# Gate one-hots from bf16 comparisons over eight tokens, in a hybrid conv / RWKV-7 / PEER layer

## The chip, the cores and the metric

The kernel runs on one core of one Trainium2 chip, as one launch. The metric is the device time of that core in microseconds (us). Besides plain runs there is one profiled execution, whose trace is read here. Engines are called by the profile's names: PE (matmuls), PEld (weight loads), DVE (VectorE), ACT (ScalarE), POOL (GpSimd), SP (the queue that issues most DMAs). "L1028" is line 1028 of the kernel before.

## The reference, cut to what matters

One layer for 1024 tokens of width 1024. A token-mixing sub-layer (convolution heads and an RWKV-7 recurrence) is followed by PEER retrieval over 128 x 128 = 16384 single-neuron experts. The change lies in the second part:

```
q  = (h2 @ peer_wq) per head (8 heads), split into two halves
s1 = q[:half] . peer_k1   (128 keys)      s2 = q[half:] . peer_k2   (128 keys)
v1, i1 = top_k(s1, 16);   v2, i2 = top_k(s2, 16)
sc, ci = top_k(all 256 sums v1[i] + v2[j], 16)
experts = i1[ci // 16] * 128 + i2[ci % 16];   gates = softmax(sc)
z   = h2 . peer_u[experts];   act = gelu(z) * gates
y2  = sum over the 8 x 16 chosen experts of act * peer_v[experts]
```

So each token has 128 chosen experts, each with a first key (0 to 127), a second key (0 to 127) and a gate.

## The kernel before

**Two ways through PEER.** Tokens are cut into eight tiles of 128. Tiles 5, 6, 7 (`GT`) gather their chosen rows by indirect DMA. Tiles 0 to 4 (`DT`, 640 tokens) go the dense way: all 16384 experts are computed by matmuls, and the result is multiplied by a gate matrix that is zero except at the chosen experts. The gate matrix of a token is 128 x 128 (first key by second key). It is built as a product of two one-hot matrices over the 128 choices k of the token: `oa[k, e] = (first key of k == e)` and `ob[k, e] = gate of k * (second key of k == e)`; a matmul over k gives the matrix.

**Stages.** First the input projection and the convolution; then the RWKV recurrence over 16 chunks, into which other work is filled in as generators (`fill`); then what is left of that work; last, from about 1380 us on, the dense experts (line 1250 on: 32 groups with matmuls at L1268 and L1302) with the gathers beside them. The work filled in, in order of its emission: `front` (output projection and norms of 256 tokens), `query` (query projection, scores, and `best16`: top 16 on DVE), `choose` (from the two top 16 to experts and gates of one tile, on the list `slow`), and `gate_matrix` (list `gates`, one step per four tokens). Lines 600 and 1111 set how often a gate step is emitted; a scheduler orders each engine's instructions by emission and priority, and gate steps after the recurrence get a raised priority (`GPRI`).

**choose** (L917). Positions become keys by a lookup as a one-hot sum: `oh = (iota_q == sel)` (L968, bf16), times the key (L971), summed over 16 places. On POOL (`E is G`, the tiles below token 512) the sum is a tree of four adds (L977, L979); on DVE (`E is V`: tiles 4 and 5 here, and tiles 6 and 7 later in `choose_late`, two heads at a time) it is one reduction, L974. Keys and gates are stored as f32 in `sel_d` (L960), but for tile 4, whose tiles are handed over directly.

**gate_matrix** (L995). The three 128 x 128 arrays of a tile (first keys, second keys, gates; rows are tokens) are loaded into `selr` (L1006) and transposed on PE into one PSUM bank (L1012); ACT copies them to SBUF as `selt` (L1013) and negated as `selneg` (L1018). For four of the five tiles the bank (`selbank`) is kept for the tile and the keys are read from it in PSUM; for the first tile they are read from `selt` in SBUF. Then, for each four tokens ("a quad", 160 in all):

- DVE compares an f32 iota with the four first keys: `oa`, 512 elements (L1028), and with three second keys: `ob[:, :3]`, 384 elements (L1032).
- POOL multiplies these three by their gates (L1034).
- ACT makes the fourth from the iota alone: Square of (iota - key), then Relu of (gate - gate * square) (L1037, L1038).
- PE multiplies, one matmul per token (L1040), and ACT copies the result to `stage` (L1041). Each 32 tokens `stage` goes to DRAM (L1048), 2 MB at a time.

`oa` and `ob` are rings of `GB` = 3 buffers. Tiles of the stages before the experts are drawn from one ring of `NPAGE` = 31 pages of 2 KB per partition (`page`, L161).

Of the kernel before, what the change touches and what calls it, by code (L numbers as in the profile page):

```python
# [16 lines left out]
OP = mybir.AluOpType  # L17
# [48 lines left out]
RATES = 1.0, 1.0  # L66
NPAGE = 31
TSLOW = 2
TGATE = 12
CBUF = 4  # L70
GB = 3
ABUF = 6
# [13 lines left out]
def layer_kernel(ctx, tc, x, cols, c_row, cond_w, w_in, w2a2, g2, w_out, ln_rows, wq, keys, peer_u, peer_ut, peer_v, peer_vt, out):  # L86
# [16 lines left out]
    ident = const.tile([128, 128], F32)  # L103
    iota = const.tile([128, 128], F32)
    G.iota(iota, pattern=[[1, 128]], base=0, channel_multiplier=0, allow_small_or_imprecise_dtypes=True)
    eps_ln = const.tile([128, 1], F32)
# [19 lines left out]
    h2t_d = dram.tile([2, KD, 128, ND], F32, name="h2t_d")  # L126
    sel_d = dt([3, 128, 128], "sel_d", 8)
    score_d = {t: [dram.tile([128, 512], F32, name=f"score_d{t}_{g}") for g in range(4)] for t in range(6, 8)}
    split_d, fetched = {}, {}
# [787 lines left out]
    def choose(tt, val, idx, h0, nh, nb, new, E):  # L917
# [9 lines left out]
        for hh in range(0, nh, nb):  # L927
# [8 lines left out]
            for h in range(hh, hh + nb):  # L936
                best16(top[:, h], pos[:, h], cand[:, h - hh, :])
                yield

        place = pos.bitcast(I32)  # L940
        V.tensor_scalar(m1, place, 32.0, None, op0=OP.is_ge)
# [17 lines left out]
        yield  # L959
        put = lambda w, t: None if tt == DT[-1] else ld(sel_d[tt][w][:, h0 * TOPK:h0 * TOPK + n], t.rearrange("p h r -> p (h r)"))  # L960
        for half, sel in ((0, isel), (1, jsel)):
            ib = qb[:, 2 + half]
            A.activation(ib, idx[:, :, half, :], AF.Copy)
            for hh in range(0, nh, nb):
                hs = slice(hh, hh + nb)
                oh = new("oh", BF, nb * TOPK * TOPK).rearrange("p (h q r) -> p h q r", h=nb, q=TOPK)
                sh4 = [128, nb, TOPK, TOPK]
                V.tensor_tensor(oh, iota_q[:, None].to_broadcast(sh4), sel[:, hs, None, :].to_broadcast(sh4),  # L968
                                op=OP.is_equal)
                yield  # L970
                E.tensor_mul(oh, oh, ib[:, hs, :, None].to_broadcast(sh4))  # L971
                yield
                if E is V:
                    V.tensor_reduce(fo[half][:, hs], oh.rearrange("p h q r -> p h r q"), axis=AX.X, op=OP.add)  # L974
# [20 lines left out]
    def gate_matrix(tt, chosen):  # L995

        three = lambda nm: gb[0].tile([128, 3, 128], F32, name=nm)
        quad_ = lambda nm: gb[0].tile([128, 4, 128], F32, name=nm, bufs=GB)
        st = three("selt")
        if chosen:  # L1000
            s = [t.rearrange("p h r -> p (h r)") for t in chosen]
        else:
            kept_ = three("selr")
            s = [kept_[:, w] for w in range(3)]
            for w in range(3):
                ld(s[w], sel_d[tt][w])  # L1006

        selbank.append(selbank.pop(0))
        pt = (selbank[0].tile([128, 512], F32, tag="mgate", name="selbank", bufs=1) if selbank[0] else mgate())[:, :384]
        pt = pt.rearrange("p (w t) -> p w t", w=3)  # L1010
        for w in range(3):
            T.transpose(pt[:, w], s[w], ident)  # L1012
        A.activation(st, pt, AF.Copy)  # L1013
        i1, i2, gt = (st[:, w] for w in range(3))
        if selbank[0]:
            i1, i2 = pt[:, 0], pt[:, 1]
        neg = three("selneg")
        A.activation(neg, pt, AF.Copy, scale=-1.0)  # L1018
        for r0 in range(0, 128, TB):
# [5 lines left out]
            for q in range(0, TB, 4):  # L1025
                ts = slice(r0 + q, r0 + q + 4)
                oa, ob = quad_("oa"), quad_("ob")
                V.tensor_tensor(oa, iota[:, None, :].to_broadcast([128, 4, 128]),  # L1028
                                i1[:, ts, None].to_broadcast([128, 4, 128]), op=OP.is_equal)
                pt = mgate().rearrange("p (t e) -> p t e", t=4)  # L1030

                V.tensor_tensor(ob[:, :3], iota[:, None, :].to_broadcast([128, 3, 128]),  # L1032
                                i2[:, ts.start:ts.start + 3, None].to_broadcast([128, 3, 128]), op=OP.is_equal)
                G.tensor_mul(ob[:, :3], ob[:, :3], gt[:, ts.start:ts.start + 3, None].to_broadcast([128, 3, 128]))  # L1034
                c, o = slice(ts.start + 3, ts.start + 4), ob[:, 3, :]

                A.activation(o, iota, AF.Square, bias=neg[:, 1, c])  # L1037
                A.activation(o, o, AF.Relu, bias=gt[:, c], scale=neg[:, 2, c])  # L1038
                for t in range(4):
# [17 lines left out]
    for c in range(16):  # L1057
# [3 lines left out]
        if c == 9:  # L1061
# [4 lines left out]
            fet.close()  # L1066
            gb.append(fex.enter_context(tc.tile_pool(name="gb", bufs=1)))
        if c < 14:
            flight.append([solve(c + 2)])
# [302 lines left out]
```

## Time and profile before

| what | value |
|---|---|
| three runs | 3225.85, 3225.45, 3225.2 us; median 3225.45 |
| profiled execution | 3225.41 us; its span in the trace 3223.5 us |
| granted TensorE clock, mean | 0.953 |
| busy, share of the span | PE 93%, PEld 80%, DVE 80%, ACT 37%, POOL 56% |
| L1028, 160 comparisons | 117.1 us of DVE, between 864 and 1400 us |
| L1032, 160 comparisons | 91.9 us of DVE |
| L974, 8 reductions, tiles 4 and 5 | 15.9 us of DVE, between 1316 and 1363 us |

The share of a whole span is an average over stages with different limits, so the prediction reads the stage in which the gate matrix is built: how busy each engine is there, and which wait ends last. Idle time of an engine that doesn't bind costs nothing. Rows with "x8" are groups of eight instructions; "<-" after a row's idle time names what released the engine.

### The profile page before, as it was taken

To read this page: it belongs to the slowest core of one execution; us is meant where nothing else is said; L and a number is where in the kernel's file an instruction comes from. 1 tells how busy PE (TensorE), PEld (TensorE's weight loads), DVE (VectorE), ACT (ScalarE), POOL (GpSimd) and SP (SyncE) were. 2 spreads that over 40 slices of the span, in tenths; PEclk is the share of its full clock that TensorE was granted. 3 is DMA by queue.
4 is the path that set the end of the run, shared out by engine and by line. 5 is a ranking of instruction groups with operands and counts; after the bars stand their busy time and mean duration, and the time that the engine had idled before them with its cause. 6 is when DMAs were issued, how large, how long until landed. Compare 5 with 4: busy or idle time off the path is not lost.

```text
span 3223.5 us, 53860 instructions
## 1 busy us (share of the span) xinstructions
PE 2995.2 (93%) x19952; PEld 2582.2 (80%) x19952; DVE 2563.2 (80%) x5612; ACT 1198.1 (37%) x2314; POOL 1796.7 (56%) x1408
## 2 busy tenths in 40 slices
PE   6968999899799589899999999999999999999995
PEld 4735677478688479899899988899989898999994
DVE  6279566856977979958999999898878777778788
ACT  5562344253353467552223232322323232222222
POOL 2410011133441853367777776787878777787872
PEclk9979899979699799999999999999999999999997
DMA  8876465378566898999999989899999999999994
GB/s 307 290 208 229 135 179 170 113 235 288 169 193 240 266 307 253 311 350 329 340 336 328 341 317 321 307 336 347 339 335 339 346 328 354 329 345 330 344 339 171
DMA packets 411782, 922.30 MB, mean 286 GB/s; under 512 B 81744, under 2 KB 221568, under 8 KB 389504
## 3 DMA queue, kind: packets, MB, share of 16 engines
q1 hardware_dynamic: 218688, 474.23, 43.2%
q0 software_dynamic: 110592, 402.70, 33.8%
q10 hardware_dynamic: 82240, 41.94, 4.6%
q8 instruction: 156, 2.56, 0.3%
q14 instruction: 106, 0.87, 0.1%
HBM read 788.91 MB, written 129.85 MB: 285 GB/s over the span
## 4 chain that ended last, share of the span: by engine, by line
PE 46%; DVE 13%; DMA 3%; issue 2%; ACT 1%; POOL 1%; SPq 0%; ACTq 0%; DVEq 0%; POOLq 0%
PE mg L1268 22%; PE md L1302 21%; DVE grow L1194 2%; PE mgate L1040 2%; DVE yacc L1307 1%; DVE gy L1201 1%; DMA vraw<-peer_vt 1%; PE mm L194 1%; DMA G_d<-stage 1%; DVE oa L1028 1%; DVE ob L1032 1%; DMA grow<-peer_v,eid 0%; DVE tkg L974 0%; DVE oh L968 0%; DVE bnst L202 0%
## 5 line engine op out<-in xcount | busy, mean ns | idle before, releaser
L1268 PE MATMUL mg<-h2h,uhi 128*128 128x320 f32 x2024 | 626.1, 309 | 8.0 <-DVE al L1274 8.0
L1268 PE MATMUL mg<-h2l,uhi 128*128 128x320 f32 x2024 | 625.1, 309 | 0.0
L1268 PE MATMUL mg<-h2h,ulo 128*128 128x320 f32 x2024 | 624.9, 309 | 0.0
L1201 DVE SCALAR_TENSOR_TENSOR gy<-grow,gz,gy 128x1024 f32<-128x1024 f32 x381 | 487.7, 1280 | 19.1 <-DMA grow<-peer_v,eid 17.3
L1302 PE MATMUL md<-vhi,al 128*128 128x512 f32 x1280 | 497.9, 390 | 0.0
L1302 PE MATMUL md<-vlo,ah 128*128 128x512 f32 x1280 | 496.5, 390 | 0.0
L1302 PE MATMUL md<-vhi,ah 128*128 128x512 f32 x1280 | 491.7, 391 | 4.1 <-DVE yacc L1307 2.1
L1194 DVE SCALAR_TENSOR_TENSOR grow<-grow,gh 128x1024 f32<-128x1024 f32 x384 | 460.6, 1210 | 25.6 <-DMA grow<-peer_u,eid 24.2
L1186 POOL DMA_INDIRECT grow<-peer_u,eid x384 | 363.1, 946 | 187.3 <-DVE grow L1194 78.4
L1186 POOL DMA_INDIRECT grow<-peer_v,eid x384 | 361.9, 942 | 187.6 <-DVE gy L1201 99.4
L1268 PEld LDWEIGHTS mg<-h2h,uhi 128*128 128x128 f32 x2024 | 379.9, 188 | 16.8 <-DVE al L1274 11.5
L1268 PEld LDWEIGHTS mg<-h2l,uhi 128*128 128x128 f32 x2024 | 379.9, 188 | 4.6
L1268 PEld LDWEIGHTS mg<-h2h,ulo 128*128 128x128 f32 x2024 | 379.9, 188 | 3.2
L1229 POOL TENSOR_TENSOR vlo<-vraw,vhi 128x1024 fp32r<-128x1024 f32 x128 | 309.0, 2414 | 32.4 <-ACT vhi L1227 30.0
L1229 POOL TENSOR_TENSOR ulo<-uraw,uhi 128x1024 fp32r<-128x1024 f32 x128 | 309.1, 2415 | 29.9 <-ACT uhi L1227 27.9
L1307 DVE TENSOR_TENSOR yacc<-md,yacc 128x512 f32<-128x512 f32 x310 | 210.6, 685 | 124.9 <-PE md L1302 124.3
L1302 PEld LDWEIGHTS md<-vhi,ah 128*128 128x128 f32 x1280 | 239.6, 188 | 53.1 <-ACT ah L1273 4.0
L1034 POOL TENSOR_TENSOR ob<-ob,selt 128x384 f32<-128x384 f32 x160 | 144.9, 907 | 241.7 <-DVE ob L1032 163.4
L1302 PEld LDWEIGHTS md<-vlo,ah 128*128 128x128 f32 x1280 | 240.3, 188 | 48.6
L1227 ACT ACTIVATE vhi<-vraw 128x1024 fp32r<-128x1024 f32 x128 | 135.2, 1056 | 387.8 <-DMA vraw<-peer_vt 369.9
L1302 PEld LDWEIGHTS md<-vhi,al 128*128 128x128 f32 x1280 | 240.3, 188 | 45.1 <-DVE al L1274 0.2
L182 POOL TENSOR_TENSOR wsplit<-wraw,wsplit 128x1024 fp32r<-128x1024 f32 x46 | 112.6, 2450 | 221.0 <-ACT wsplit L181 214.3
(404 smaller groups left out, 5916.8 us busy)
## 6 DMA issues: line engine op xcount, KB each, us to landing
uraw<-peer_ut SPq DMA_DIRECT2D x128, 512.0 KB, 7.1
vraw<-peer_vt SPq DMA_DIRECT2D x128, 512.0 KB, 5.5
wsplit<-split_wq SPq DMA_DIRECT2D x48, 1024.0 KB, 6.7
G_d<-stage ACTq DMA_DIRECT2D x20, 2048.0 KB, 13.6
gmat<-G_d SPq DMA_DIRECT2D x32, 1024.0 KB, 8.1
cw<-cond_w SPq DMA_DIRECT2D x48, 512.0 KB, 5.0
wsplit<-split_w_out SPq DMA_DIRECT2D x24, 1024.0 KB, 5.9
split_w_in<-wsplit SPq DMA_DIRECT2D x22, 1024.0 KB, 5.1
```

The lines of the kernel that those rows point to most:

```text
L182: G.tensor_sub(lo, raw, hi.bitcast(F32))
L194: T.matmul(pt, l[:, k, :], r[k], start=i == 0, stop=i == 3 * KD - 1)
L1034: G.tensor_mul(ob[:, :3], ob[:, :3], gt[:, ts.start:ts.start + 3, None].to_broadcast([128, 3, 128]))
L1040: T.matmul(pt[:, t, :], ob[:, t, :], oa[:, t, :], start=True, stop=True)
L1186: G.indirect_dma_start(out=r, out_offset=None, in_=peer_u if k < 128 else peer_v, in_offset=bass.IndirectOffsetOnAxis(ap=eid[:, k % 128:k ...
L1194: V.scalar_tensor_tensor(r, r, 1.0, ht, op0=OP.mult, op1=OP.mult, accum_out=z[:, i:i + 1])
L1201: V.scalar_tensor_tensor(y, r, z[:, i - 128:i - 127], y, op0=OP.mult, op1=OP.add)
L1227: A.activation(hi, raw, AF.Copy)
L1229: G.tensor_sub(lo, raw, hi.bitcast(F32))
L1268: T.matmul(p, l[:, k, :], r[k][:, bs], start=i == 0, stop=i == 3 * KD - 1)
L1302: T.matmul(p, l[:, ts], r[:, e % 2, :], start=e == 0 and q == 0, stop=e == 3 and q == 2)
L1307: ins = V.tensor_add(ya, p, ya)
```

## The change

It rewrites how the one-hots are made:

- `choose` for dense tiles writes the keys as bf16 (`fo` in `qb`) and stores them in a new bf16 array `keyb_d`. The sum over places is now the tree of adds on DVE too where a tile's eight heads are done at once; the reduction stays only in `choose_late`.
- `gate_matrix` loads bf16 keys and f32 gates into a slot of the `ob` ring, transposes the keys in bf16 into the bank, and keeps them there as bf16 (for the first tile a bf16 copy in SBUF, `selk2`). Only the gates are copied to SBUF; the negated copy goes.
- DVE compares a bf16 iota, laid out as expert by eight tokens (`iota_e`), with the keys of eight tokens: two comparisons of 1024 bf16 elements, `mask`, for eight tokens, one per key half.
- ACT copies four tokens of the first mask to f32 `oa`. POOL multiplies three tokens of the second mask with the gates into `ob`. ACT makes the fourth as a Copy with the gate as scale.
- `oa` has two buffers instead of three, `mask` has three; there are 30 pages instead of 31. The f32 iota moves out of the constants; for the masks a second one is made once, in a page.

```
-NPAGE = 31
+NPAGE = 30
-GB = 3
+GB = 2, 3
+MB = 3
...
+    keyb_d = [dram.tile([2, 128, 128], BF, name=f"keyb_d{i}") for i in range(8)]
...
+        dense = tt in DT
...
+        if dense:
+            fo = qb[:, 4], qb[:, 5]
...
-                if E is V:
+                if nh < NH:
                     V.tensor_reduce(fo[half][:, hs], oh.rearrange("p h q r -> p h r q"), axis=AX.X, op=OP.add)
                     continue
...
+            got = quad_("ob", GB[1]).rearrange("p t e -> p (t e)")
+            kb = got.bitcast(BF)[:, 0:256].rearrange("p (w k) -> p w k", w=2)
+            sg = got[:, 128:256]
+            k1, k2 = kb[:, 0], kb[:, 1]
+            ld(kb, keyb_d[tt].rearrange("w p k -> p w k"))
+            ld(sg, sel_d[tt][2])
...
+        keys_ = pt.bitcast(BF)[:, 0:256].rearrange("p (w k) -> p w k", w=2)
+        for w, k in enumerate((k1, k2)):
+            T.transpose(keys_[:, w], k, identb)
+        T.transpose(pt[:, 128:256], sg, ident)
+        gt = gb[0].tile([128, 128], F32, name="selt")
+        A.activation(gt, pt[:, 128:256], AF.Copy)
+        if not selbank[0]:
+            both = gb[0].tile([128, 2, 128], BF, name="selk2")
+            A.activation(both, keys_, AF.Copy)
+            keys_ = both
...
-                V.tensor_tensor(oa, iota[:, None, :].to_broadcast([128, 4, 128]),
-                                i1[:, ts, None].to_broadcast([128, 4, 128]), op=OP.is_equal)
+                if q % 8 == 0:
+                    masks = []
+                    for w in range(2):
+                        m = gb[0].tile([128, 128, 8], BF, name="mask", bufs=MB)
+                        V.tensor_tensor(m, iota_e, keys_[:, w, None, r0 + q:r0 + q + 8].to_broadcast([128, 128, 8]),
+                                        op=OP.is_equal)
+                        masks.append(m)
+                ma, mb = (m[:, :, q % 8:q % 8 + 4].rearrange("p e t -> p t e") for m in masks)
+                oa, ob = quad_("oa", GB[0]), quad_("ob", GB[1])
+                A.activation(oa, ma, AF.Copy)
+                c = r0 + q
+                G.tensor_mul(ob[:, :3], mb[:, :3], gt[:, c:c + 3, None].to_broadcast([128, 3, 128]))
+                A.activation(ob[:, 3], mb[:, 3], AF.Copy, scale=gt[:, c + 3:c + 4])
...
-                V.tensor_tensor(ob[:, :3], iota[:, None, :].to_broadcast([128, 3, 128]),
-                                i2[:, ts.start:ts.start + 3, None].to_broadcast([128, 3, 128]), op=OP.is_equal)
-                G.tensor_mul(ob[:, :3], ob[:, :3], gt[:, ts.start:ts.start + 3, None].to_broadcast([128, 3, 128]))
...
-                A.activation(o, iota, AF.Square, bias=neg[:, 1, c])
-                A.activation(o, o, AF.Relu, bias=gt[:, c], scale=neg[:, 2, c])
...
+            iota_e = gb[0].tile([128, 128, 8], BF, name="iota_e")
+            V.tensor_copy(iota_e, iota[:, :, None].to_broadcast([128, 128, 8]))
```

More of the change, by code (lines that the diff above doesn't have):

```diff
@@ L103, in layer_kernel @@
     ident = const.tile([128, 128], F32)
-    iota = const.tile([128, 128], F32)
-    G.iota(iota, pattern=[[1, 128]], base=0, channel_multiplier=0, allow_small_or_imprecise_dtypes=True)
     eps_ln = const.tile([128, 1], F32)
@@ L152, in layer_kernel @@
     iota_q = const.tile([128, TOPK, TOPK], BF, name="iota_q")
+    iota = fe.tile([128, 128], F32, name="iota")
+    G.iota(iota, pattern=[[1, 128]], base=0, channel_multiplier=0, allow_small_or_imprecise_dtypes=True)
     V.tensor_copy(iota_q, iota[:, :TOPK, None].to_broadcast([128, TOPK, TOPK]))
@@ L959, in choose @@
         yield
-        put = lambda w, t: None if tt == DT[-1] else ld(sel_d[tt][w][:, h0 * TOPK:h0 * TOPK + n], t.rearrange("p h r -> p (h r)"))
+        if dense:
+            fo = qb[:, 4], qb[:, 5]
+        put = lambda w, t: None if tt == DT[-1] else ld((keyb_d if dense and w < 2 else sel_d)[tt][w][:, h0 * TOPK:h0 * TOPK + n],
+                                                        t.rearrange("p h r -> p (h r)"))
         for half, sel in ((0, isel), (1, jsel)):
@@ L995, in gate_matrix @@
     def gate_matrix(tt, chosen):
-        three = lambda nm: gb[0].tile([128, 3, 128], F32, name=nm)
-        quad_ = lambda nm: gb[0].tile([128, 4, 128], F32, name=nm, bufs=GB)
-        st = three("selt")
+        iota_e, identb = gb[1:]
+        quad_ = lambda nm, bufs: gb[0].tile([128, 4, 128], F32, name=nm, bufs=bufs)
         if chosen:
-            s = [t.rearrange("p h r -> p (h r)") for t in chosen]
+            k1, k2, sg = [t.rearrange("p h r -> p (h r)") for t in chosen]
         else:
[L1003 to L1006, printed above, removed]
-        selbank.append(selbank.pop(0))
[L1009 to L1018, printed above, removed]
+            got = quad_("ob", GB[1]).rearrange("p t e -> p (t e)")
[4 more added lines that the diff above has]
+            ld(sg, sel_d[tt][2])
+        selbank.append(selbank.pop(0))
+        pt = selbank[0].tile([128, 512], F32, tag="mgate", name="selbank", bufs=1) if selbank[0] else mgate()
+        keys_ = pt.bitcast(BF)[:, 0:256].rearrange("p (w k) -> p w k", w=2)
[8 more added lines that the diff above has]
+            keys_ = both
         for r0 in range(0, 128, TB):
@@ L1067, in layer_kernel @@
             gb.append(fex.enter_context(tc.tile_pool(name="gb", bufs=1)))
+            iota = page("iota", w=128)
+            G.iota(iota, pattern=[[1, 128]], base=0, channel_multiplier=0, allow_small_or_imprecise_dtypes=True)
+            iota_e = gb[0].tile([128, 128, 8], BF, name="iota_e")
+            V.tensor_copy(iota_e, iota[:, :, None].to_broadcast([128, 128, 8]))
+            identb = gb[0].tile([128, 128], BF, name="identb")
+            V.tensor_copy(identb, ident)
+            gb.extend((iota_e, identb))
         if c < 14:
```

3 lines of the change are left out of this document (removed).

## The prediction, made before the changed kernel had run

> **What bounds the kernel now.** I read the page first for the shares, then the windows view, to find where VectorE (DVE) is the engine that is never idle, then the same windows for line 1028 alone, to see how much of the changed work lies in each. Columns of the first view: window, its length, busy us (and instructions) of PE, PE's weight loads, DVE, ACT and POOL, then the granted TensorE clock, the DMA share and GB/s.
>
> ```profile
> span 3223.5 us, 53860 instructions
> ```
> ```profile
> 300.00:820.00 520.00, 485.99 (x4634) 356.15 (x4632) 350.20 (x913) 204.64 (x412) 109.93 (x67) 0.90 0.60 191
> 820.00:1000.00 180.00, 160.16 (x1901) 140.41 (x1899) 153.46 (x486) 88.43 (x206) 84.06 (x83) 0.86 0.55 179
> 1000.00:1050.00 50.00, 45.31 (x389) 36.53 (x389) 37.07 (x215) 13.65 (x32) 7.10 (x7) 0.93 0.73 252
> 1050.00:1100.00 50.00, 25.43 (x125) 21.31 (x123) 49.72 (x140) 23.14 (x47) 39.46 (x36) 0.77 0.78 247
> 1100.00:1250.00 150.00, 126.85 (x925) 120.17 (x925) 125.97 (x389) 92.36 (x218) 83.69 (x89) 0.91 0.93 302
> 1250.00:1370.00 120.00, 105.15 (x849) 101.75 (x849) 118.58 (x362) 78.68 (x192) 45.49 (x46) 0.96 0.85 276
> 1370.00:1405.00 35.00, 33.02 (x260) 32.00 (x259) 19.50 (x35) 27.56 (x65) 17.14 (x19) 0.99 1.03 349
> 1405.00:3223.00 1818.00, 1770.31 (x9923) 1610.57 (x9921) 1516.71 (x2684) 515.92 (x847) 1342.92 (x1024) 0.99 0.91 328
> ```
>
> The last 1818 us are the expert matmuls, PE busy 97% of them; the change touches no instruction there. Everything is decided before 1405, where the gate matrix is built beside the last projections. DVE is full in two windows, 49.7 of 50 and 118.6 of 120. Between them (1100 to 1250) DVE has 24 us idle, and the DMA engines carry 0.93 of their time. At the end, PE (33 of 35) and DMA are full.
>
> Line 1028 runs once for four tokens (a "quad"), so its count says how many quads each window holds:
>
> ```profile
> 820.00:1000.00 180.00, 30.80 (x32) 0.86 0.55 179
> 1050.00:1100.00 50.00, 6.02 (x9) 0.77 0.78 247
> 1100.00:1250.00 150.00, 36.38 (x54) 0.91 0.93 302
> 1250.00:1370.00 120.00, 31.61 (x47) 0.96 0.85 276
> 1370.00:1405.00 35.00, 11.65 (x17) 0.99 1.03 349
> ```
>
> **The price of a comparison.** DVE's groups between 820 and 1405 us (line, engine, operation, out<-in, shapes, count | busy, mean ns | idle before), then a stretch of its timeline (start, us), then single lines (count: min/median/max ns, first and last start):
>
> ```profile
> L1028 DVE TENSOR_TENSOR oa<-iota,selbank 128x512 f32<-128x512 f32 x128 | 86.3, 674 | 28.0 <-PE mgate L1040 27.6 <-ACT selneg L1018 0.2
> L1032 DVE TENSOR_TENSOR ob<-iota,selbank 128x384 f32<-128x384 f32 x128 | 69.6, 544 | 0.0
> ```
> ```profile
> 1348.83 2.35 DVE L971 TENSOR_TENSOR oh<-oh,tkb 128x1024 bf16<-128x1024 bf16 x2
> 1351.10 0.67 DVE L1028 TENSOR_TENSOR oa<-iota,selbank 128x512 f32<-128x512 f32 x1
> 1351.70 0.54 DVE L1032 TENSOR_TENSOR ob<-iota,selbank 128x384 f32<-128x384 f32 x1
> 1352.16 2.98 DVE L971 TENSOR_TENSOR oh<-oh,tkb 128x1024 bf16<-128x1024 bf16 x2
> 1356.12 4.05 DVE L974 TENSOR_REDUCE tkg<-oh 128x64 f32<-128x1024 bf16 x2
> 1360.09 0.67 DVE L1028 TENSOR_TENSOR oa<-iota,selbank 128x512 f32<-128x512 f32 x1
> ```
> ```profile
> L1028 DVE TENSOR_TENSOR oa<-iota,selbank x128: 630/675/690, 1003.8 to 1399.1; 128x512 f32<-128x512 f32 x128
> ...
> L1028 DVE TENSOR_TENSOR oa<-iota,selt x32: 647/693/2415, 864.1 to 994.1; 128x512 f32<-128x512 f32 x32
> ```
> ```profile
> L968 DVE TENSOR_TENSOR oh<-iota_q,tkb x24: 677/684/2400, 824.1 to 1347.6; 128x1024 bf16<-128x1024 bf16 x24
> L968 DVE TENSOR_TENSOR loh<-iota_q,ltkb x16: 404/416/1252, 1540.9 to 2141.6; 128x512 bf16<-128x512 bf16 x16
> ```
>
> A quad costs DVE 1.06 us from start to start (1351.10 to 1352.16; neighbours overlap by 0.075 us), so eight tokens cost 2.12. After the change eight tokens cost two bf16 comparisons of 1024 elements. The trace has that shape twice. L968 compares a bf16 iota with bf16 keys that run contiguously, both in SBUF: 0.684 us (median), 0.61 after the overlap. L971 has an operand repeated along the innermost axis: 2.27 us for two (1348.83 to 1351.10), 1.135 each. So the same 1024 bf16 elements cost 0.61 or 1.135. The new comparison reads runs of eight contiguous keys and a contiguous iota, which is L968's pattern, but its keys lie in PSUM for four of the five tiles (selbank, 128 of the 160 quads), and no row of before has a bf16 operand in PSUM. An f32 comparison loses nothing by a PSUM operand: 675 ns with selbank, 693 with selt in SBUF (medians). I take 0.61 because the access pattern is L968's, and keep 1.135 as the other end. Saved per quad: (2.12 - 1.22)/2 = 0.45 us; at the other end (2.27 - 2.12)/2 = 0.075 us is lost.
>
> The Trainium skill speaks against this: "VectorE: DVE Perf Modes", section "The perf-mode tier table (the rule you actually need)", puts a tensor_tensor with any PSUM operand at one element per cycle. The section on PSUM operands below it caps them only at the packed two-element mode, and no run here shows which holds. By the tier table the sum would be the first rival's.
>
> **The lookup sums.**
>
> ```profile
> L974 DVE TENSOR_REDUCE tkg<-oh x8: 1972/2018/2109, 1315.8 to 1363.1; 128x64 f32<-128x1024 bf16 x8
> ```
>
> Eight reductions, 1.985 us each from start to start (1356.12 to 1360.09 is two), become four adds each on DVE, of 512, 256, 128 and 64 outputs. From the two L968 rows, 512 elements more cost 268 ns; so 0.416, 0.28, 0.215 and 0.18, less four overlaps: 0.80 us. But an add reads two SBUF tensors, and such instructions stretch beside POOL:
>
> ```profile
> L968 DVE TENSOR_TENSOR oh<-iota_q,tkb 128x1024 bf16<-128x1024 bf16 x8 | 6.9, 916 | 0.0
> ```
> ```profile
> L1034 POOL TENSOR_TENSOR ob<-ob,selt x160: 818/827/2817, 867.4 to 1400.4; 128x384 f32<-128x384 f32 x160
> ```
> ```profile
> 1308.64 2.35 DVE L971 TENSOR_TENSOR oh<-oh,tkb 128x1024 bf16<-128x1024 bf16 x2
> ...
> 1308.86 2.82 POOL L1034 TENSOR_TENSOR ob<-ob,selt 128x384 f32<-128x384 f32 x1 [3.53 <-DVE ob L1032]
> ```
>
> Between 1250 and 1370 L968 averages 0.916 us instead of 0.684, and the POOL multiply at 1308.86, usually 0.83 us, lasted 2.82 beside two L971. With 0.2 us more per add, a reduction's replacement costs 1.6; I take 0.38 saved, 3 us for the eight. Ends: 9.4 us saved (no collision), 4 us lost (each add waits for half a POOL multiply of 0.83 us). All eight lie in the window 1250 to 1370.
>
> **ACT and POOL.** ACT's groups between 820 and 1405, and the two rows nearest to its new work (ns min/median/max):
>
> ```profile
> L1041 ACT ACTIVATE stage<-mgate 128x512 f32<-128x512 f32 x160 | 94.7, 592 | 89.9 <-PE mgate L1040 83.3 <-DMA wsplit<-split_wq 6.2
> L1038 ACT ACTIVATE ob<-ob,selt,selneg 128x128 f32<-128x128 f32 x160 | 77.0, 494 | 17.5 <-DMA G_d<-stage 13.4 <-ACT ob L1037 1.2 <-DMA selr<-sel_d 1.0
> L1037 ACT ACTIVATE ob<-iota,selneg 128x128 f32<-128x128 f32 x160 | 62.9, 397 | 9.6 <-PE mgate L1040 9.4
> ```
> ```profile
> L486 ACT ACTIVATE ctap<-ident,colt x104: 381/389/403, 223.1 to 613.1; 128x128 f32<-128x128 f32 x104
> L800 ACT ACTIVATE ychi<-ycf x16: 612/630/633, 542.8 to 1109.7; 128x512 fp32r<-128x512 f32 x16
> ```
>
> Per quad ACT loses Square and Relu (0.397 + 0.494) and gains a 512-element copy (0.63, L800) and a Copy with a column scale (0.389, L486): 0.13 us more. In the window 1250 to 1370 that is 47 x 0.13 = 6 us on 78.7, under PE's 105; at nothing. If strided bf16 reads took ACT twice as long, it would be 0.76 per quad, 114 us, and ACT would bind; L1041 reads four strided tokens at the same 0.59 us as a dense copy, which speaks against it. The copy also puts ACT between DVE and the matmul, beside POOL's multiply of 0.83 us, which ends later. POOL's multiply keeps its 384 elements; only an operand turns bf16. The negated copy (L1018, five times) goes. iota_e, identb and the second iota are made once, about 2 us of DVE where it has 27 us idle (820 to 1000).
>
> **Loads and pages.** The three loads of a tile's selection become two, into a slot of the ob ring instead of a buffer of their own. The chain has, in order of time:
>
> ```profile
> 1141.75 3.98 PE mgate L1040 x18
> 1145.85 1.17 SPq L1006
> 1147.08 8.95 DMA selr<-sel_d
> ```
>
> So the load already starts when the last matmuls of the tile before are done, and takes 9 us there. Now SP also waits for one of three ob slots, a quad's time (2.6 us: 47 in 120), and behind it on SP's queue stand the weight tiles of the projections (L175), three deep. Bounds: 0 to 3 x 2.6 = 8 us for the three such tiles; I take 3, because one load fewer gives part back. The page ring falls from 31 to 30. No row of before prices a page; if the ring paced all of 300 to 1100, one page in 31 would be 26 us, and nothing if it paces none of it. I take 2, near the low end: PE is busy 93% of 300 to 820.
>
> **The sum, by window.**
> - 820 to 1000: the first tile, keys in SBUF. DVE has 27 us idle: -1.
> - 1050 to 1100: DVE full, PE, ACT and DMA at half to three quarters: all 9 x 0.45 = 4 us count: -4.
> - 1100 to 1250: 54 x 0.45 = 24 us go from an engine with 24 us idle, while DMA has some 10 us left (0.93 of 150): -3.
> - 1250 to 1370: 47 x 0.45 + 3 = 24 us go from a full DVE; next is PE with 105. At the density of the last window (33.02 of 35) PE needs 105.15/0.943 = 111.5: -8.5.
> - 1370 to 1405: PE and DMA are full: 0.
> - Loads +3, page +2.
>
> Together -11.5. The profiled execution took 3225.41 us (its span 3223.5 and 1.9 around it), the median of the three runs is 3225.45: both give 3214.
>
> **Rivals.** (1) *The packed rate doesn't come with keys in PSUM*, so the comparisons don't do what they are there for. 0.075 us per quad is added: 0.7 in the first full window, 3.5 - 3 in the second; the first tile still gains 1; loads and page 5: 3231, inside what can be told from no change. For it: no row with such an operand. Against: the pattern is L968's.
> (2) *DMA and PE hide it.* Only the 4 us of 1050 to 1100 come, loads and page take them back: 3226. For it: DMA at 0.93 and 1.03 around, and an ACT that fills up where DVE empties. Against: DMA has 0.85 in the window that holds most of the gain.
> (3) *The page ring paces the front*, before any gate work. Its place is 300 to 1100, its price up to 26 us in place of my 2, so 3238. It decides from about 18 us on, where the whole gain and 6.5 more are gone. For it: projections, the convolution and the selection all draw from this one ring. Against: PE is idle only 34 us of the 520 from 300 to 820.
>
> **How the numbers follow.** A measurement of this kernel can tell about 0.2% from no change, 6.5 us: the borders are 3219 and 3232. Chances: forecast 0.50 (nearly all under 3219), rival 1 0.22 (mostly between, a little above), rival 2 0.12, rival 3 0.16. Faster 0.49, same 0.30, slower 0.21. The low end of the range is every DVE saving of the full windows counted with 10 us more from the middle and no page cost: -4 - 24 - 10 + 3 - 1 = -36, cut to 3194 since PE is 88% busy there already; the high end takes in rival 3: 3240. The forecast's own range is 3196 to 3222.
>
> **What would show it.** Right: comparisons of 1024 bf16 with PSUM keys near 0.69 us, DVE under 90% in 1250 to 1370, the first expert matmuls some 10 us earlier, the part after them as long as now (1818 us). Wrong: comparisons near 1.2 us (rival 1); the same DVE saving, but the window as long, with DMA or ACT full (2); a later start of the gate work and PE idle well over 34 us between 300 and 820 (3). An ACT copy of 512 over 0.7 us would move the bound to ACT.

## The result, and the profile after

The changed kernel takes 3259.25 us (median of four runs, 3257.43 to 3264.67), the kernel before 3225.32 (four runs, 3224.54 to 3225.85): ratio 1.0115, 95% interval 1.0095 to 1.0135. It is 34 us slower; the forecast was 11.5 us faster, and the range ended at 3240. The profiled execution took 3259.26 us. Its span, and its windows in the columns of the prediction:

```profile
span 3257.2 us, 53740 instructions
```
```profile
300.00:820.00 520.00, 493.91 (x4755) 361.13 (x4754) 358.61 (x931) 208.03 (x420) 120.92 (x72) 0.92 0.60 197
820.00:1000.00 180.00, 156.91 (x1853) 137.54 (x1852) 132.08 (x444) 106.50 (x200) 82.70 (x80) 0.86 0.50 163
...
1050.00:1100.00 50.00, 24.58 (x90) 20.10 (x89) 49.84 (x126) 25.91 (x40) 42.24 (x34) 0.66 0.72 234
1100.00:1250.00 150.00, 122.52 (x863) 113.87 (x863) 94.49 (x294) 121.97 (x206) 84.19 (x86) 0.91 0.87 283
1250.00:1370.00 120.00, 105.60 (x834) 101.15 (x832) 99.61 (x365) 101.26 (x178) 47.41 (x43) 0.96 0.80 266
1370.00:1405.00 35.00, 22.36 (x153) 20.82 (x154) 8.17 (x12) 23.83 (x40) 11.54 (x12) 0.85 0.85 277
1405.00:3223.00 1818.00, 1796.02 (x10081) 1636.85 (x10079) 1487.36 (x2631) 533.39 (x874) 1354.33 (x1035) 1.00 0.91 329
```

DVE did lose its work: 94 of 150 instead of 126, and 100 of 120 instead of 119. But ACT rose from 92 to 122 of 150 and from 79 to 101 of 120, and neither PE nor DMA took up the time that DVE gave back. From 1370 to 1405, where PE had been full (33 of 35), it now does 22. The same two middle windows for the copy to `stage` alone (L1050, one per quad) count the quads that were finished:

```profile
1100.00:1250.00 150.00, 30.29 (x50) 0.91 0.87 283
1250.00:1370.00 120.00, 25.46 (x43) 0.96 0.80 266
```

93 quads, against 100 of the same copy (54 and 46) before. Where the loss ends up is seen at the expert matmuls into the bank `mg`, first of the changed kernel and then of the one before (ns min/median/max, first and last start). A few expert matmuls into another bank, `md`, run earlier, between gate matmuls; the first into `mg` starts when the last gate matmul has started (1433.4 and 1402.7 us), so it marks the end of the gate stage (to some 2 us in the other kernels), and "the first expert matmul" means this one from here on:

```profile
L1284 PE MATMUL mg<-h2h,uhi x2024: 302/309/636, 1433.4 to 3197.0; 128*128 128x320 f32 x184
```
```profile
L1268 PE MATMUL mg<-h2h,uhi x2024: 302/309/418, 1402.8 to 3162.0; 128*128 128x320 f32 x184
```

It starts 30.6 us later. From there to the end of the span it is 1823.8 us against 1820.7: 31 of the 34 us are lost before the experts, in the gate stage. Its groups, 820 to 1480 us:

```profile
L1043 ACT ACTIVATE oa<-mask 128x512 f32<-128x512 bf16 x160 | 183.0, 1147 | 15.3 <-DVE mask L1038 9.8 <-PE mgate L1049 5.4
...
L1045 POOL TENSOR_TENSOR ob<-mask,selt 128x384 f32<-128x384 bf16 x160 | 168.8, 1069 | 250.5 <-DVE mask L1038 140.0 <-PE mgate L1049 78.7 <-DVE tkg L781 10.8
L1050 ACT ACTIVATE stage<-mgate 128x512 f32<-128x512 f32 x160 | 95.6, 600 | 22.5 <-PE mgate L1049 21.5 <-DMA wsplit<-split_wq 0.5
L1038 DVE TENSOR_TENSOR mask<-iota_e,selbank 128x1024 bf16<-128x1024 bf16 x128 | 86.2, 681 | 100.4 <-ACT ob L1046 50.3 <-ACT oa L1043 41.8 <-POOL ob L1045 6.8
L1046 ACT ACTIVATE ob<-mask,selt 128x128 f32<-128x128 bf16 x160 | 82.7, 534 | 49.6 <-DVE mask L1038 43.6 <-DMA h2t_d<-h2lo 5.9
```

Read two columns. The mean: the comparison of 1024 bf16 with keys in PSUM takes 681 ns, so the packed rate is there; ACT's copy takes 1147 instead of the 630 that the forecast took, its column 534 instead of 389. ACT has 1147 + 534 + 600 = 2281 ns per quad; before it had 397 + 494 + 592 = 1483, and 0.63 + 0.389 + 0.592 = 1.61 us was forecast. The idle time: DVE stands 100 us before the comparisons, and 92 of them end with an ACT instruction that reads a mask. The chains of waits from 1100 to 1390, before and after, say the same in shares (the answer cuts the line off):

```profile
by line: PE mgate L1040 14.5%; PE mm L194 11.5%; DMA G_d<-stage 9.8%; DVE oa L1028 6.5%; DVE ob L1032 5.5%; DVE tkg L974 4.5%; issue 4.1%; DMA wsplit<-split_wq 3.1%; DMA selr<-sel_d 3.1%; DVE oh L971 3.0%; DVE xt L837 2.7%; PE mm L891 2.3%;
```
```profile
by line: ACT oa L1043 15.5%; ACT stage L1050 8.7%; ACT ob L1046 7.0%; DMA G_d<-stage 6.9%; PE mm L196 6.3%; issue 5.1%; DVE mask L1038 4.8%; PE mgate L1049 4.1%; DVE oh L977 3.5%; DVE rnew L211 3.3%; DVE oh L983 2.8%; DVE oh L974 2.3%; DMA 
```

Before, PE's matmuls lead; after, three ACT lines hold 31%.

### The profile page after: what moved, and what is told of

Same layout as the page of the kernel before. It is cut to its first block, busy times and chain, and to the rows that moved or that the text cites. A ratio compares the mean times of both kernels' runs of the same rounds, so it can differ in the third digit from the quotient of the medians.

```text
span 3257.2 us, 53740 instructions
## 1 busy us (share of the span) xinstructions
PE 3007.5 (92%) x19952; PEld 2593.2 (80%) x19952; DVE 2496.2 (77%) x5478; ACT 1306.9 (40%) x2312; POOL 1822.8 (56%) x1409
## 4 chain that ended last, share of the span: by engine, by line
PE 57%; DVE 17%; DMA 6%; ACT 6%; issue 4%; POOL 2%; SPq 0%; another core or an unknown queue 0%; ACTq 0%; POOLq 0%; DVEq 0%
PE mg L1284 21%; PE md L1318 20%; PE mm L196 6%; DVE cacc L482 2%; DVE grow L1210 2%; ACT oa L1043 2%; PE mm L490 1%; DMA grow<-peer_v,eid 1%; ACT stage L1050 1%; PE mm L821 1%; DVE gy L1217 1%; DVE cw L267 1%; PE mgate L1049 1%; DMA G_d<-stage 1%; ACT ob L1046 1%
## 5 line engine op out<-in xcount | busy, mean ns | idle before, releaser
L1210 DVE SCALAR_TENSOR_TENSOR grow<-grow,gh 128x1024 f32<-128x1024 f32 x384 | 460.9, 1212 | 29.7 <-DMA grow<-peer_u,eid 15.9
L1045 POOL TENSOR_TENSOR ob<-mask,selt 128x384 f32<-128x384 bf16 x160 | 168.8, 1069 | 250.5 <-DVE mask L1038 140.0
L1049 PE MATMUL mgate<-oa,ob 128*128 128x128 f32 x1280 | 194.1, 301 | 62.2 <-ACT oa L1043 44.9
```

The costliest lines, as they stand in the source:

```text
L1045: G.tensor_mul(ob[:, :3], mb[:, :3], gt[:, c:c + 3, None].to_broadcast([128, 3, 128]))
L1049: T.matmul(pt[:, t, :], ob[:, t, :], oa[:, t, :], start=True, stop=True)
L1210: V.scalar_tensor_tensor(r, r, 1.0, ht, op0=OP.mult, op1=OP.mult, accum_out=z[:, i:i + 1])
```

## The experiments

Four theories are named in the expectations. A: ACT's read of the masks binds the gate stage. B: the page ring. C: the key loads, which now go through the `ob` ring. D: three mask buffers are too few. On these chips the kernel before had medians of 3219 to 3225 us, and single runs of one kernel spread over some 20 us (before: 3212 to 3234), so each kernel is compared by its ratio to the runs of before beside it. A profile is one such run, and each kernel has one, so a difference of a few us between two profiles can be chance.

### ACT's read made dense

```
-A.activation(oa, ma, AF.Copy)
+A.activation(oa, masks[0].rearrange("p e t -> p (e t)")[:, 64 * (q % 8) * 2:64 * (q % 8) * 2 + 512].rearrange("p (t e) -> p t e", t=4), AF.Copy)
-A.activation(ob[:, 3], mb[:, 3], AF.Copy, scale=gt[:, c + 3:c + 4])
+A.activation(ob[:, 3], masks[1].rearrange("p e t -> p (e t)")[:, 128 * (q % 8):128 * (q % 8) + 128], AF.Copy, scale=gt[:, c + 3:c + 4])
```

> The changed kernel, each instruction in the same order on every engine; only ACT's two reads of a mask (the copy to oa and the scaled column of ob) take contiguous bf16 elements instead of every eighth, so the elements go to the wrong tokens and the output is not the layer's. Theory A (reading every eighth bf16 element slows ACT, and ACT then binds the gate stage): the copy falls from 1.15 to about 0.63 us, the column from 0.53 to about 0.39, ACT's load by some 105 us, and the time to 3214-3232. Theory B (one page less paces the front) and theory C (loads of keys through the ob ring hold SP's queue): those are untouched, so 3250-3262. Theory D (three mask buffers are too few for DVE, whatever ACT costs): DVE still waits some 100 us for masks, 3245-3262.

3236.78 us (nine runs), ratio 1.0037 (1.0024 to 1.005): 22 us of the 34 are gone with nothing but the addresses of ACT's reads changed. The groups:

```profile
L1043 ACT ACTIVATE oa<-mask 128x512 f32<-128x512 bf16 x160 | 99.9, 626 | 15.5 <-DVE mask L1038 7.7 <-PE mgate L1049 7.4
...
L1038 DVE TENSOR_TENSOR mask<-iota_e,selbank 128x1024 bf16<-128x1024 bf16 x128 | 85.7, 680 | 80.3 <-ACT ob L1046 40.6 <-ACT oa L1043 29.1 <-POOL ob L1045 9.9
```

The copy costs 626 ns, as forecast for a dense one. The first expert matmul starts at 1412.9 us, 20.5 earlier than in the changed kernel and 10 later than before, and the time is above the 3214 to 3232 of theory A: something of the loss is left. DVE still waits 80 us for mask buffers, but that alone doesn't show a loss: a later run, with the masks in halves, has 87 us of this wait and a gate stage that ends earlier than before.

### The page alone

```
-NPAGE = 31
+NPAGE = 30
```

> The kernel before with 30 pages instead of 31 and nothing else. Theory A: 3220-3232, the page costs a few us at most. Theory B: 3240-3260, most of the 34 us is the page's. C and D: as A.

3250.85 us, ratio 1.0076 (1.0053 to 1.01), which looks like theory B. But the first expert matmul:

```profile
L1268 PE MATMUL mg<-h2h,uhi x2024: 302/309/636, 1400.6 to 3186.6; 128*128 128x320 f32 x184
```

It starts at 1400.6 us, no later than with 31 pages (1402.8). The loss lies after it: 3251.6 - 1400.6 = 1851 us against 1820.7. The changed kernel has 30 pages and 1823.8 there, so this loss isn't its own; why the kernel before has it with 30 pages stays open. In this profile the page delays neither the front nor the gate stage, so theory B falls for these.

### The same reads, walked in runs of four

```
-A.activation(oa, ma, AF.Copy)
+A.activation(oa.rearrange("p t e -> p e t"), masks[0][:, :, q % 8:q % 8 + 4], AF.Copy)
```

> The changed kernel, but ACT's copy to oa walks expert by expert: it reads runs of four adjacent bf16 elements and writes f32 at a stride, the same values to the same places. If it is the stride between 2-byte elements that ACT pays for, the copy falls to 0.63-0.8 us and the time to 3225-3240 (the column of ob stays at 0.53). If any access that isn't fully contiguous costs, the copy stays near 1.15 and the time at 3255-3262. Theories B, C, D: 3250-3262 in either case.

3248.57 us, ratio 1.0073 (1.005 to 1.0096); the copy:

```profile
L1043 ACT ACTIVATE oa<-mask 128x512 f32<-128x512 bf16 x160 | 178.8, 1122 | 14.9 <-DVE mask L1038 9.5 <-PE mgate L1049 5.4
```

The copy is hardly cheaper (1122 instead of 1147; the time is 24 us above before instead of 34), but now the f32 writes are strided (512 bytes apart), so this alone doesn't tell reading from writing. The next one does.

### Rows laid out expert by token

```
+oa = oa.rearrange("p t e -> p (t e)").rearrange("p (e t) -> p e t", t=4)
-A.activation(oa, ma, AF.Copy)
+A.activation(oa, masks[0][:, :, q % 8:q % 8 + 4], AF.Copy)
-T.matmul(pt[:, t, :], ob[:, t, :], oa[:, t, :], start=True, stop=True)
+T.matmul(pt[:, t, :], ob[:, t, :], oa[:, :, t], start=True, stop=True)
```

> The changed kernel with oa laid out as expert by token: ACT reads runs of four adjacent bf16 elements and writes contiguously; the matmuls read their moving operand at a stride of four f32. The same values. In the runs-of-four run the writes were strided, so this tells reading from writing. If only reading single elements at a stride is slow, the copy is 0.6-0.8 us and the time 3233-3242, as in the dense-read run, unless PE's matmuls (0.30 us now) get longer. If runs of four are as slow to read, the copy stays near 1.1 and the time is 3245-3260.

3313.97 us, ratio 1.0274 (1.0248 to 1.03). Groups up to 1480 us:

```profile
L1050 PE MATMUL mgate<-oa,ob 128*128 128x128 f32 x1223 | 299.6, 406 | 18.2 <-ACT oa L1044 10.4 <-POOL ob L1046 7.8
...
L1044 ACT ACTIVATE oa<-mask 128x512 f32<-128x512 bf16 x154 | 95.9, 625 | 18.7 <-PE mgate L1050 12.2 <-DVE mask L1038 5.7 <-ACT stage L1051 0.7
```

The same mask elements, read four neighbours at a time and written densely, cost 625 ns. So ACT pays for single bf16 elements 16 bytes apart (1147) and for strided writes (1122). Here the stride went to PE, whose matmul takes 406 ns instead of 301 with f32 values 16 bytes apart.

### Masks for the second key only

First keys are compared in f32 by DVE as before; ACT's copy goes. With one mask per eight tokens instead of two, the ring has two buffers.

```
-MB = 3
+MB = 2
...
-for w in range(2):
+for w in (1,):
...
-A.activation(oa, ma, AF.Copy)
+V.tensor_tensor(oa, iota_f[:, None, :]..., keys_[:, 0, r0 + q:r0 + q + 4, None]..., op=OP.is_equal)
```

> The changed kernel with bf16 masks for the second keys alone; the first keys are compared by DVE straight into f32 oa, four tokens at a time, as before (f32 iota, bf16 keys in PSUM), so ACT has no copy to oa. DVE per eight tokens 2 x 0.60 + 0.61 = 1.81 us (2.12 before, 1.22 changed), ACT per quad 0.60 + 0.53 = 1.13 (1.49 before, 2.28 changed). Theory A: 3205-3226, at or below the kernel before. B and C: 3245-3262. D: in between, since only one mask per eight tokens is drawn, from two buffers.

3221.57 us, ratio 0.9997 (0.9982 to 1.0013): as before. ACT has 0.53 + 0.59 = 1.12 us per quad, and the loss is gone.

> The second-key-only run with one difference: a tile's keys and gates are loaded into a buffer of their own instead of a slot of the ob ring. Theory C (the load waits for the ring, so the next tile's transposes come only at the end of a tile): the transposes of tiles 2 and 3 come earlier than the last quads of the tile before, and the time falls by 3-10 us to 3211-3219. If the load's wait is hidden: 3217-3226.

The same with a buffer for the loaded keys (`got = gb[0].tile([128, 256], F32, name="keyr")` in place of the `ob` slot): 3226.76 us, ratio 1.0004 (0.9991 to 1.0016). The loads did wait for the ring: the last transposes of keys loaded through the `ob` slot start at 1254.3 us, with a buffer of their own at 1163.0. But no time is gained, and the kernel that loads through the slot has no loss either: theory C falls as a cause of the 34 us.

### The lookup sums alone

The kernel before, with `if nh < NH:` in place of `if E is V:`.

> The kernel before with one part of the change alone: the lookup sums of tiles 4 and 5 are trees of adds on DVE in place of the eight reductions. Theory A: some 4 us of DVE fall away in the window that is full, 3215-3226. If the adds collide with POOL and stand in the way of the gate comparisons: 3226-3240, and a part of what the dense-read run still lacks against the kernel before is theirs.

3226.87 us, ratio 1.0013 (1.0 to 1.0027). In its profile, a run of 3216.52 us and so the fastest of the ten, the first expert matmul starts at 1387.1 us, 15.7 earlier than before; the median shows none of it.

### Finer masks, with dense reads and with the real ones

Both have masks of four tokens in six buffers, the same bytes as three of eight; the second leaves all reads as the changed kernel's code has them. With four tokens a mask, neighbours along the experts lie 8 bytes apart instead of 16.

```
-MB = 3
+MB = 6
-m = gb[0].tile([128, 128, 8], BF, name="mask", bufs=MB)
+m = gb[0].tile([128, 128, 4], BF, name="mask", bufs=MB)
```

> The dense-read run (its output is not the layer's) with masks of four tokens, 512 elements, in a ring of six: the same bytes, given back after one quad instead of two. DVE pays 0.68 instead of 0.61 us per quad. Theory D (DVE waits for masks, 99 us of idle before comparisons in the dense-read run, and the quads with it): the idle falls under 50 us and the time to 3222-3232. If what is left has another cause: 3232-3245.

3222.61 us, ratio 0.9996 (0.9985 to 1.0007). The time is the one that theory D expected; the idle time is not, DVE still waits 66 us before these comparisons instead of under 50. POOL's multiply, whose values now lie 8 bytes apart, has fallen from 1069 to 868 ns, so the ring isn't all that differs from the dense-read kernel.

> The changed kernel with masks of four tokens in six buffers instead of eight tokens in three; ScalarE reads single bf16 values at a stride of four elements (8 bytes). Against the run with dense reads and fine masks this differs in ScalarE's read alone. Theory A: ScalarE's copy of 512 still takes about 1.1 us and the time is 3238 to 3252; if the price hangs on the length of the stride (16 bytes), the copy takes 0.6 to 0.85 us and the time is 3220 to 3230. Theory D, that the coarse ring is the whole loss, gives 3225 whatever the copy takes.

3221.14 us, ratio 0.9995 (0.998 to 1.001). Its groups:

```profile
L1045 POOL TENSOR_TENSOR ob<-mask,selt 128x384 f32<-128x384 bf16 x160 | 138.8, 870 | 246.0 <-PE mgate L1049 115.1 <-DVE mask L1038 73.1 <-DVE gs L749 12.8
L1043 ACT ACTIVATE oa<-mask 128x512 f32<-128x512 bf16 x160 | 108.0, 675 | 18.5 <-DVE mask L1038 9.9 <-PE mgate L1049 8.6
L1038 DVE TENSOR_TENSOR mask<-iota_e,selbank 128x512 bf16<-128x512 bf16 x256 | 98.5, 410 | 63.3 <-ACT oa L1043 54.1 <-ACT selt L1022 8.0 <-ACT ob L1046 0.4
```

The copy takes 675 ns, not the 1.1 us that theory A expected of any stride: the price hangs on the distance of 16 bytes. (Only bf16 was tried, so bytes and elements aren't told apart.) But for the comparison over eight tokens, everything that the change wants is in this kernel, and it is as fast as the kernel before.

### POOL's read made dense too

The dense-read kernel, with POOL's operand `mb[:, :3]` replaced by 384 contiguous elements.

> The changed kernel with ScalarE's reads of the masks made contiguous, as in the dense-read run, and with GpSimd's multiply reading the mask contiguously as well; masks still of eight tokens in three buffers. The rows so made are not the gates' one-hots, so the output is not the layer's. Theory A says that single bf16 values read at a stride cost time on ScalarE and, to a smaller part, on GpSimd (its multiply 1069 ns at a stride of eight elements, 868 at a stride of four); theory D says that what is left of the loss, 11 us of the dense-read run, is the coarse ring of three masks of eight tokens. If A: the multiply falls to 830 to 900 ns and the time to 3222 to 3230. If D: the multiply gets cheaper and the time stays at 3232 to 3242.

3240.64 us, ratio 1.0058 (1.0037 to 1.008).

```profile
L1045 POOL TENSOR_TENSOR ob<-mask,selt 128x384 f32<-128x384 bf16 x160 | 144.4, 912 | 260.0 <-PE mgate L1049 107.0 <-DVE mask L1038 103.8 <-PE mm L196 14.9
...
L1038 DVE TENSOR_TENSOR mask<-iota_e,selbank 128x1024 bf16<-128x1024 bf16 x128 | 86.0, 680 | 81.3 <-ACT ob L1046 38.5 <-ACT oa L1043 31.7 <-POOL ob L1045 8.8
```

POOL's multiply falls to 912 ns, and the time is no better than with ACT's reads alone. The profile divides it:

```profile
L1284 PE MATMUL mg<-h2h,uhi x2024: 302/309/635, 1405.1 to 3178.4; 128*128 128x320 f32 x184
```

The gate stage ends at 1405.1 us, 7.8 earlier than with ACT's reads alone and 2.3 later than before. The loss lies behind it, 3240.8 - 1405.1 = 1836 us against 1820.7, as with 30 pages. So the time is the one that theory D expected, but POOL's read isn't excluded as a part of what the dense-read kernel lost in its gate stage.

### ACT loaded without any of the change

The kernel before, with its copy to `stage` done twice (`A.activation(stage[:, :, q:q + 4], pt..., AF.Copy)` repeated), so about 2.1 us of ACT per quad, nearly the 2.28 of the changed kernel.

> The kernel before with ScalarE's copy of the gate rows from PSUM done twice: ScalarE has 1.49 + 0.60 = 2.09 us for four tokens instead of 1.49, and nothing of the change is in it (f32 comparisons, no masks, no strided read). Theory A, that ScalarE's load alone can hold up the gate stage: 3238 to 3252, the first expert matmul 12 to 25 us later than 1402.8. If ScalarE's load only matters together with the masks' ring (D): 3222 to 3230.

3241.98 us, ratio 1.0058 (1.0036 to 1.008). Its first expert matmul, and groups of PE and ACT in its gate stage:

```profile
L1269 PE MATMUL mg<-h2h,uhi x2024: 302/309/636, 1410.4 to 3181.8; 128*128 128x320 f32 x184
```
```profile
L1040 PE MATMUL mgate<-oa,ob 128*128 128x128 f32 x1280 | 190.7, 298 | 64.2 <-POOL ob L1034 38.0 <-ACT stage L1042 22.6 <-ACT yo L764 1.4
...
L1041 ACT ACTIVATE stage<-mgate 128x512 f32<-128x512 f32 x160 | 97.1, 607 | 78.9 <-PE mgate L1040 76.1 <-DMA G_d<-stage 2.5
L1042 ACT ACTIVATE stage<-mgate 128x512 f32<-128x512 f32 x160 | 96.9, 607 | 0.1
```

0.6 us more of ACT per quad, with no mask and no strided read of one, costs 21 us. But only 7.6 us of it lie before the first expert matmul, not the 12 to 25 that theory A expected; the part behind it is 3242.1 - 1410.4 = 1832 us, 11 longer than before. So by this profile a load on ACT does delay the gate stage, although ACT is idle 79 us before its first copy, but nearly the changed kernel's load delays it by a quarter of the 31 us. The rest needs something that this kernel hasn't: ACT's place between DVE and PE, the masks that it holds while it reads them, or POOL's slower multiply. No run takes these one by one.

### The second key with finer masks

Four-token masks in the second-key kernel, four buffers; meant as the best version.

> The kernel with bf16 masks for the second keys alone, these masks of four tokens in four buffers. For four tokens VectorE has about 0.68 + 0.41 us, ScalarE 1.13, GpSimd about 0.87 instead of 1.156. Theory A (engines that read the masks at a stride pay for it): GpSimd's multiply near 870 ns, the gate stage ends 8 to 20 us earlier than before, 3208 to 3220 with the expert stage as long as in the other runs. If the end of the gate stage is set by PE and the key loads: 3220 to 3226.

3237.51 us (nine runs), ratio 1.0048 (1.0031 to 1.0064): outside both expectations. POOL's multiply is 931 ns, and in the profile the first expert matmul starts at 1396.4, 6.4 us earlier than before; the loss lies after it. Its cause stays open.

### Eight tokens in halves, and fewer fine masks

The changed kernel with one edit, the order of a mask's elements (the iota and the keys are addressed to match); then the fine masks with `MB = 3`.

```
-m = gb[0].tile([128, 128, 8], BF, name="mask", bufs=MB)
+m = gb[0].tile([128, 2, 128, 4], BF, name="mask", bufs=MB)
-ma, mb = (m[:, :, q % 8:q % 8 + 4].rearrange("p e t -> p t e") for m in masks)
+ma, mb = (m[:, q % 8 // 4].rearrange("p e t -> p t e") for m in masks)
```

> The changed kernel with its eight-token masks laid out as two halves of four tokens, all values right: still one comparison for eight tokens and three mask buffers, but ScalarE and GpSimd read at a stride of 8 bytes instead of 16. Theory A (ScalarE's price hangs on the stride's length): the comparison stays near 0.68 us, ScalarE's copy falls from 1147 to about 675 ns, GpSimd's multiply from 1069 to about 870, and the time falls by about the 22 us that the dense read gave, to 3230 to 3242, what is left being the eight-token ring (theory D). If the eight-token ring costs nothing: 3220 to 3226. If the comparison loses its packed rate by this layout (over 1.1 us): 3240 or more.

3224.76 us (ten runs), ratio 1.0017 (1.0005 to 1.003): 5.6 us above the runs of before beside it, instead of 34. Its groups, two windows, and its chain from 1100 to 1390:

```profile
L1046 POOL TENSOR_TENSOR ob<-mask,selt 128x384 f32<-128x384 bf16 x160 | 141.7, 897 | 241.6 <-DVE mask L1038 110.2 <-PE mgate L1050 84.6 <-ACT oa L1044 13.6
L1044 ACT ACTIVATE oa<-mask 128x512 f32<-128x512 bf16 x160 | 107.0, 671 | 12.3 <-DVE mask L1038 9.0 <-PE mgate L1050 3.3
...
L1038 DVE TENSOR_TENSOR mask<-iota_e,selbank 128x1024 bf16<-128x1024 bf16 x128 | 85.7, 679 | 86.9 <-ACT ob L1047 39.7 <-ACT oa L1044 31.4 <-POOL ob L1046 8.2
L1047 ACT ACTIVATE ob<-mask,selt 128x128 f32<-128x128 bf16 x160 | 62.7, 408 | 41.6 <-DVE mask L1038 39.2 <-DVE cand L934 1.5 <-POOL xt L854 0.8
```
```profile
1100.00:1250.00 150.00, 128.77 (x964) 122.23 (x965) 98.43 (x362) 102.89 (x221) 70.41 (x82) 0.93 0.95 311
1250.00:1370.00 120.00, 102.03 (x816) 99.06 (x815) 88.95 (x305) 85.08 (x193) 46.72 (x50) 0.93 0.86 287
```
```profile
by line: PE mgate L1050 15.7%; PE mm L196 14.2%; DMA G_d<-stage 6.2%; DVE mask L1038 5.6%; ACT oa L1044 4.3%; issue 3.3%; PE mm L821 3.2%; DMA wsplit<-split_wq 2.9%; ACT stage L1051 2.8%; POOL ob L1046 2.6%; PE md L1285 2.5%; PE mm L893 2.4
```

The comparison is unchanged (679 ns), ACT has 671 + 408 + 594 = 1673 ns per quad, and PE's matmuls lead the chain again. The first expert matmul starts at 1399.2, 34 us earlier than in the changed kernel and 3.6 earlier than before; the part behind it is 1822.2 us. The two `oa` buffers, the page, the loads through the `ob` slot and the three masks of eight tokens are all still in it, so none of them is the cause of the late gate stage.

> The run with masks of four tokens, but with three buffers for them instead of six: as many masks as in the changed kernel, each for half as many tokens. Theory D, too few masks ahead of their readers: the comparisons wait for ScalarE and GpSimd as in the dense-read run, 3232 to 3245. If the loss is that one mask is held for two groups of four tokens: 3220 to 3228.

3233.08 us, ratio 1.0045 (1.0028 to 1.0062): 14 us above before, where six buffers cost nothing.

```profile
L1043 ACT ACTIVATE oa<-mask 128x512 f32<-128x512 bf16 x160 | 107.6, 672 | 25.5 <-DVE mask L1038 23.0 <-PE mgate L1049 2.5
...
L1038 DVE TENSOR_TENSOR mask<-iota_e,selbank 128x512 bf16<-128x512 bf16 x256 | 102.5, 413 | 81.2 <-ACT oa L1043 61.2 <-POOL ob L1045 8.0 <-ACT ob L1046 7.4
```

DVE waits 81 us for masks to come free instead of 63, and ACT waits 23 us for DVE instead of 10: with three buffers the two engines take turns. The first expert matmul starts at 1407.3 instead of the 1396.4 of six buffers. Theory D holds for this ring, whose three masks hold half as many tokens as those of the change.

## Why the prediction was wrong

**The step that failed** is "ACT and POOL": "Per quad ACT loses Square and Relu (0.397 + 0.494) and gains a 512-element copy (0.63, L800) and a Copy with a column scale (0.389, L486): 0.13 us more ... at nothing." Both rows that gave the prices are dense f32 reads. The new reads take single bf16 elements 16 bytes apart, and cost 1.147 and 0.534: 0.79 us more per quad, not 0.13. The prediction had the case in hand ("If strided bf16 reads took ACT twice as long, it would be 0.76 per quad ... and ACT would bind") and dismissed it by L1041, "four strided tokens at the same 0.59 us". But L1041 reads PSUM, and writes to SBUF four neighbours at a time; it says nothing on a strided read of SBUF. So the case had no chance of its own, and the range, up to 3240, left no room for it. Its marker did work: "an ACT copy of 512 over 0.7 us would move the bound to ACT". POOL's multiply was put at nothing in the same way ("only an operand turns bf16"); it went from a median of 827 ns to 1021.

The Trainium skill had a rule for it. "SBUF — State Buffer", section "Door 1: The DMA port swizzle (why `[64,N]` ≈ `[32,N]`)", says that SBUF is read in lines of 16 bytes, that the full rate takes at least two accesses to each line, and that every new line costs. The runs agree with that: two elements in each 16 bytes cost 675 ns, one costs 1147. The same place in the Trainium skill lists eight bf16 as a free stride, which is these 16 bytes; there the measurement decides against it. The Trainium skill's "GPSIMD Engine Reference", section "7. Performance pitfalls for Q7 kernels", puts the border above 8 bytes, with about half more time per element: POOL's multiply agrees on the border (870 ns at 8 bytes, 1069 at 16) and shows 23% more.

**Also missing**: what slower readers do to the masks. The prediction put a busy share under another's (ACT's 79 + 6 us under PE's 105) as cover. ACT isn't full in any window even now (122 of 150); what it delays is the return of mask buffers and PE's operands, and DVE, PE and ACT then wait in turn. The profiles place the loss (one profile each; us):

| kernel | first expert matmul | from there to the end |
|---|---|---|
| before | 1402.8 | 1820.7 |
| changed | 1433.4 | 1823.8 |
| ACT's reads dense | 1412.9 | 1821.7 |
| ACT's and POOL's reads dense | 1405.1 | 1835.7 |
| eight tokens in halves | 1399.2 | 1822.2 |
| fine masks, three buffers | 1407.3 | 1823.4 |
| fine masks, six buffers | 1396.4 | 1832.0 |
| stage copy twice | 1410.4 | 1831.7 |

The layout of the masks accounts for the late end of the gate stage: with the halves all of it is gone, with ACT's dense reads two thirds. Of the 34 us of time the halves take away 28 and the dense reads 22. The 6 us that the halves keep (1.0005 to 1.003) are not in the gate stage of their profile, and their cause stays open. A ring too short costs time as well, as the fine masks show (three buffers 14 us, six nothing); the changed kernel's own three masks of eight tokens delay the gate stage of no profile once ACT and POOL read them at 8 bytes, although DVE still stands 87 us before its comparisons. The part behind the gate stage, which the change doesn't touch, is up to 15 us longer in some of these profiles, and 30 with the page alone; what makes it so stays open.

**What was right.** The price of the comparison: 681 ns with keys in PSUM, 0.69 forecast, so rival 1 falls. This decides the point on which the Trainium skill's "VectorE: DVE Perf Modes" spoke against the change. Its section "The perf-mode tier table (the rule you actually need)" has one element per cycle for a tensor_tensor with a PSUM operand, and its section on PSUM operands below caps them at the packed two-element mode. The runs bear out the second: medians of 686 ns with keys in PSUM, 693 with keys in SBUF. The lookup sums:

```profile
L983 DVE TENSOR_TENSOR oh<-oh 128x512 bf16<-128x512 bf16 (+2 forms) x24 | 8.6, 419 | 0.0
L985 DVE TENSOR_TENSOR tkg<-oh 128x64 f32<-128x64 bf16 x4 | 2.1, 552 | 0.0
```

With four more adds of 64 that is 11.5 us for 15.9: 4.4 saved, 3 forecast. DVE under 90% from 1250 to 1370 (83%), though in part because it stands waiting. The experts' part as long as before, to 3 us. Rival 3 falls by its own sign: from 300 to 820 PE is idle 26 us, not well over 34, and the gate work starts no later (first gate matmul at 866.0 us, 868.7 before). The loads at little: the last transposes of loaded keys start at 1253.3 us instead of 1168.5, where the prediction had a load wait a quad's time, but a buffer of their own gained no time. The page is not shown to be cheap everywhere: alone it made the kernel before 26 us slower, behind the gate stage, where the changed kernel doesn't lose them.

**By windows.** The 4 us counted from 1050 to 1100 didn't come: DVE is as full there as before (49.84 of 50). The last matmul of the output projection (L819, now L821), which stands behind this work, starts at 1147.7 us instead of 1137.7. The last projection matmul (L194, now L196) starts at 1400.6 instead of 1376.0: the 3 and 8.5 us counted in the two middle windows turned into a loss. With the masks in halves the two start at 1135.7 and 1373.4, so the layout made it.

**Would the forecast have come with cheap reads?** No. With fine masks the time is that of before, with the real reads (0.998 to 1.001) and with dense ones (0.9985 to 1.0007). In the profile of the latter, a run of 3225.15 us, the first expert matmul starts at 1392.5, 10 us earlier than before, as forecast, but the part after it takes 3223.1 - 1392.5 = 1831 us instead of 1820.7. That is rival 2 in its outcome (3226 us), though not shown to be its mechanism: why a gate stage that ends earlier isn't followed by an earlier end stays open. No version was faster than the kernel before by more than the runs can tell.

## What to carry to other kernels

Price a read by a row with the same memory, element size and stride: a cheap strided read of PSUM says nothing about one of SBUF, and a layout that suits the engine that writes can nearly double the time of the engine that reads. When work moves from a full engine to one with idle time, ask which buffers the second one now holds, and who waits for it: a reader that is late stalls everyone although no engine is full. Before a wait is called the loss, look for a kernel that has the wait without the loss. And place a difference by stage before giving it a cause: part of the losses here lay behind the stage that was edited. A case that you can state with its price ("twice as long, and ACT would bind") belongs among the rivals with a chance, unless a row of the very same kind excludes it.

## What the runs showed of the hardware

- ACT, 512 bf16 elements from SBUF to f32: dense 626 to 630 ns, runs of four 625, single elements 8 bytes apart 671 to 675, 16 bytes apart 1147; 128 elements with a column scale: 396 to 398, 408 to 412, 509 to 534 (dense, 8, 16 bytes). Dense reads with f32 writes 512 bytes apart were not tried; runs of four with such writes took 1122.
- POOL, 384 elements with a bf16 operand: 912 dense, 867 to 931 at 8 bytes, 1050 to 1156 at 16 (means; they include what the engine loses beside others).
- PE: 128 columns with f32 values 16 bytes apart take 406 ns instead of 301.
- DVE, bf16 comparison with an operand in PSUM: 679 to 682 ns for 1024 elements, 410 to 413 for 512.
